# New orders of blocks in four feed-forward stages, free places asked for turned activations, earlier memory sums and shared keys and values stored in three parts

## The chip, the core and the metric

The kernel runs on one core of one Trainium2 chip. Its engines are PE (matrix products), DVE (vector), ACT (scalar), POOL (a slow general engine) and SP, which only issues DMA transfers, all on one queue and in program order. Each engine works off its own list of instructions in order and waits at the head of the list for what an instruction needs. The metric is the device time of one execution in microseconds (us); lower is better.

## What is computed

Two layers of a decoder trunk, with 256 tokens, width 1024 and 256 memory tokens. Each layer is a half-step SwiGLU feed-forward stage (FFN), a mixer, and a second FFN. Layer 0's mixer is an mLSTM with attention over the memory; layer 1's mixer (mixer B) is a dilated sliding-window attention with attention over the memory, and takes its keys and values from one projection made after layer 0.

```python
for layer in range(DEPTH):
    x = x + 0.5 * swiglu(rms_norm(x, ffn1_norm[layer]), ffn1_w_gate[layer], ffn1_w_up[layer], ffn1_w_down[layer])
    h = rms_norm(x, mix_norm[layer])
    mem_n = rms_norm(mem, mem_norm[layer])
    if layer < N_A_LAYERS:
        mix = mlstm_mixer(h, mem_n, ...)
    else:
        mix = dilated_mixer(h, mem_n, k_sh, v_sh, ...)
    x = x + mix
    x = x + 0.5 * swiglu(rms_norm(x, ffn2_norm[layer]), ...)
    if layer == N_A_LAYERS - 1:
        kv = rms_norm(x, kv_norm) @ w_kv
        k_sh, v_sh = ...
```

In `memory_cross_attention` the memory gives `kv = mem_n @ w_mem_kv`; the keys are normalised by head once more (`rms_norm` over 64 columns).

## The kernel before

**Products.** Every float32 matrix is split into a rounded high part `hi` and a remainder `lo`, and every product is three matmuls on PE: lo by high, hi by high, hi by low (`mm3`). The names show this: `gups<-lo,xh`, `gups<-hi,xh`, `gups<-hi,xl`. A token half is called t, 0 or 1.

**Weights.** They stream from DRAM in units of 128 x 1024 numbers (512 KB). SP loads a unit into one of six `raw` places, ACT casts it to `hi`, DVE subtracts it to `lo`; hi and lo stand in a ring of eight places until PE has used them. `_stream` writes down the order of the units for the whole kernel.

**FFN.** The hidden width 2816 makes eleven blocks of 256 columns. "g" with a block number is its gate and up products (into a bank of PSUM named `gups`, or `eb`, `gb`, `ub` where pieces are added up on DVE), "d" its product back to width 1024 (into `acc`). A step of two digits, such as 15 or 67, is one of seven products (first digit) of a scheme in the manner of Strassen that makes the gate and up products of two blocks, 5 and 6 or 7 and 8 (second digit 5 or 7), out of seven instead of eight; their weights are loaded as `pa` to `pd`, added and subtracted on DVE and split again, and their activations are `xs`, `xd`, `th`, `tl`. A "p" in the table is one row unit of `b_w_out` (mixer B's output matrix): it is split there, hi and lo go to DRAM as `wo`, and in mixer B two DMAs bring them back in place of a load, a cast and a subtraction.

**Turned blocks.** For d the activation `h` must stand with the hidden column on the partitions. For most blocks that is made without PE: DVE transposes h in squares of 32 into a place called `hb` (one instruction for each t), SP stores hb to DRAM (`hd`) and loads it back rearranged into a place called `ht`, then ACT casts it to `hhb` and DVE subtracts it to `hlb`, which PE reads. There are two hb places, one ht place and four places in DRAM. Both places are memory that a former user may still hold: an instruction that writes there waits for it, and holds up all behind it on its engine's list.

**Order.** `PLANS` gives the order of blocks for the four FFNs, named (layer, which): (0, 1), (0, 2), (1, 1), (1, 2). Within it the program is written by cooperative chains: each step of a chain is written down when a planner's clock, `_Model`, says that its inputs are ready on its engine; the planner's costs (`COST`, and in `_Engine` some special cases such as `pow` on POOL) decide only which instruction stands before which.

**Memory keys.** `memory_stats` loads the memory (`mt`), sums squares on ACT (`junk`) and takes the root on POOL (`memr`). `memory_kv` projects it (`mkvps`), scales by memr (`vm`, `sq` on ACT, `kn` on DVE), sums by head (`hss` on DVE), takes the root on POOL (`rp_e`, `rp_r`), multiplies kn by it on DVE and transposes it on PE (`tpk`). In layer 0 this is begun behind block 4 of FFN (0, 1).

**Shared keys and values.** `shared_kv` writes them to `kT` and `v` (traced as kTs and vs, 768 KB each); when all is done, `kept` stores both to DRAM with one DMA each, and mixer B loads them back. Their memory is used again by the next FFN, for hb among other things.

## Time and profile before

| | us |
|---|---|
| median of 3 runs | 989.51 (988.31 to 990.08) |
| the profiled execution | 989.23 |
| its span in the profile | 987.5 |
| PE busy in the span | 966.7 |
| DVE busy | 797.2 |
| ACT busy | 592.7 |

The profile lists for each engine the time in which it executes; in its timeline, matmuls of 512 columns are 0.39 us long and start 0.23 us apart, since they overlap. For an instruction that had to wait, the idle time ahead of it stands in brackets with the instruction that ended the wait.

The stages lie in the span as follows, read off the timeline: FFN (0, 1) to about 203, mixer A to 325, FFN (0, 2) to 501, the shared keys and values to 540, FFN (1, 1) to 731, mixer B to 793, FFN (1, 2) to the end.

### The profile page before, as it was taken

The numbers are of one execution on the slowest core, as the hardware profiler recorded it, in microseconds if no ns is written. First come the engines' busy times: TensorE is split into PE (matmuls) and PEld (weight loads), VectorE is DVE, ScalarE is ACT, GpSimd is POOL, SyncE is SP. The second block draws the span as 40 slices with busy tenths as digits, with TensorE's granted clock in tenths as the row PEclk, the third lists the DMA queues.
The fourth block names the chain that finished last, engine by engine and source line by source line (L and its number), as shares of the span: only waits on it lengthen the run. The fifth ranks groups of instructions, "written<-read, shape, count | busy, mean of one in ns | idle before, by whom it ended". The sixth has DMA issues, their size and how long they took to land.

```text
span 987.5 us, 13069 instructions
## 1 busy us (share of the span) xinstructions
PE 966.7 (98%) x4595; PEld 798.9 (81%) x4595; DVE 797.2 (81%) x1143; ACT 592.7 (60%) x931; POOL 49.6 (5%) x78
## 2 busy tenths in 40 slices
PE   9997999999999999999999999999999899999998
PEld 6886888899998888888878877778887678888877
DVE  5976976469896799999686799899676879898983
ACT  7664655377664756665476555665566476465651
POOL 0002000010010000000021000010002000000000
PEclk9999899999999999999999999999999999999999
DMA  9893278545455784843866866873757249468351
GB/s 355 297 384 144 86 235 298 166 146 199 128 192 193 293 302 157 304 173 121 291 186 181 324 233 226 277 271 97 258 201 262 89 165 336 159 221 313 105 182 54
DMA packets 82025, 212.40 MB, mean 215 GB/s; under 512 B 7788, under 2 KB 29224, under 8 KB 81960
## 3 DMA queue, kind: packets, MB, share of 16 engines
q1 hardware_dynamic: 81816, 211.54, 61.7%
q8 instruction: 36, 0.59, 0.2%
q14 instruction: 29, 0.24, 0.1%
q10 hardware_dynamic: 144, 0.04, 0.0%
HBM read 196.84 MB, written 14.70 MB: 214 GB/s over the span
## 4 chain that ended last, share of the span: by engine, by line
PE 73%; DVE 12%; DMA 6%; ACT 4%; issue 4%; POOL 1%; SPq 0%; DVEq 0%; ACTq 0%
PE gups L785 34%; PE acc L785 19%; DVE lo L369 6%; PE aps L785 6%; PE oacc L785 4%; PE kvps L785 3%; DMA ht<-hd 2%; DMA raw<-in_wts 2%; PE bqps L785 2%; ACT hi L369 1%; PE mkvps L785 1%; DMA kept<-vs 1%; PE tps L792 1%; DMA hd<-hb 1%; DVE hlb L369 1%
## 5 line engine op out<-in xcount | busy, mean ns | idle before, releaser
L369 DVE TENSOR_TENSOR lo<-raw,hi 128x1024 fp32r<-128x1024 f32 (+3 forms) x239 | 271.9, 1158 | 45.8 <-ACT hi L369 42.7
L369 ACT CAST hi<-raw 128x1024 fp32r<-128x1024 f32 (+3 forms) x239 | 232.9, 1002 | 50.7 <-PE gups L785 19.3
L785 PE MATMUL gups<-lo,xh 128*128 128x512 f32 x540 | 210.2, 392 | 2.8 <-DVE kn L369 1.9
L785 PE MATMUL gups<-hi,xh 128*128 128x512 f32 x540 | 209.5, 390 | 0.0
L785 PE MATMUL gups<-hi,xl 128*128 128x512 f32 x540 | 209.2, 390 | 0.0
L785 PEld LDWEIGHTS gups<-lo,xh 128*128 128x128 f32 x540 | 101.7, 188 | 25.5 <-DVE kn L369 2.3
L785 PE MATMUL acc<-lo,hhb 128*128 128x512 f32 x304 | 119.6, 393 | 0.5 <-ACT hhb L369 0.5
L785 PEld LDWEIGHTS gups<-hi,xh 128*128 128x128 f32 x540 | 101.4, 188 | 22.0 <-ACT hi L369 1.4
L785 PEld LDWEIGHTS gups<-hi,xl 128*128 128x128 f32 x540 | 101.5, 188 | 21.4
L785 PE MATMUL acc<-hi,hlb 128*128 128x512 f32 x304 | 118.6, 390 | 0.0
L785 PE MATMUL acc<-hi,hhb 128*128 128x512 f32 x304 | 118.3, 389 | 0.0
L369 DVE SCALAR_TENSOR_TENSOR lo<-raw,gains,hi 128x512 fp32r<-128x512 f32 x112 | 77.8, 744 | 9.2 <-ACT hi L369 8.6
L369 ACT ACTIVATE sil<-gups,rstd 128x256 f32<-128x256 f32 x67 | 31.6, 472 | 76.9 <-PE gups L785 76.7
L369 ACT ACTIVATE hi<-raw,gains 128x512 fp32r<-128x512 f32 x112 | 72.6, 713 | 6.0 <-DMA raw<-in_wts 2.2
L785 PEld LDWEIGHTS acc<-hi,hlb 128*128 128x128 f32 x304 | 57.1, 188 | 12.4 <-DVE hlb L369 0.4
L785 PEld LDWEIGHTS acc<-lo,hhb 128*128 128x128 f32 x304 | 57.1, 188 | 12.3 <-ACT hhb L369 0.9
L785 PEld LDWEIGHTS acc<-hi,hhb 128*128 128x128 f32 x304 | 57.1, 188 | 11.4
L369 ACT CAST hhb<-ht 128x512 fp32r<-128x512 f32 x38 | 23.5, 619 | 58.6 <-DMA ht<-hd 58.5
L785 PE MATMUL gups<-lo,th 128*128 128x512 f32 x136 | 54.2, 398 | 2.2 <-DVE gb L369 1.3
L369 DVE TENSOR_TENSOR lo<-pa,hi 128x1024 fp32r<-128x1024 f32 x42 | 51.1, 1216 | 5.3 <-ACT hi L369 4.9
L785 PE MATMUL gups<-hi,tl 128*128 128x512 f32 x136 | 53.8, 396 | 0.3 <-DVE tl L369 0.3
L785 PE MATMUL gups<-hi,th 128*128 128x512 f32 x136 | 53.7, 395 | 0.0
(237 smaller groups left out, 1594.5 us busy)
## 6 DMA issues: line engine op xcount, KB each, us to landing
raw<-in_wts SPq DMA_DIRECT2D x254, 512.0 KB, 5.2
raw<-in_wts SPq DMA_DIRECT2D x32, 384.0 KB, 3.8
hd<-hb SPq DMA_DIRECT2D x38, 256.0 KB, 5.1
ht<-hd SPq DMA_DIRECT2D x38, 256.0 KB, 4.6
pa<-in_wts SPq DMA_DIRECT2D x14, 512.0 KB, 5.1
pb<-in_wts SPq DMA_DIRECT2D x14, 512.0 KB, 6.1
pc<-in_wts SPq DMA_DIRECT2D x14, 512.0 KB, 7.0
pd<-in_wts SPq DMA_DIRECT2D x14, 512.0 KB, 5.9
```

The costliest lines, as they stand in the source:

```text
L369: call(out, *args, **kw)
L785: self.pe.matmul(out, lhsT=lhsT, rhs=rhs, start=start, stop=stop, skip_group_check=more)
L792: self.pe.transpose(out, in_, ident)
```

## The change

Five things are changed.

1. `PLANS` holds other orders for all four FFNs. Rows of `b_w_out` that are split early ("p") were two, one in (0, 2) and one in (1, 1); now they are six: one in (0, 1), four in (0, 2), one in (1, 1).
2. The hb and ht places: now two and two in (0, 1), two and one in (1, 1), three and two in the other two. A new `vacant` keeps a chain from writing down its transpose or its load until the planner holds the place to be free, and `held_by` counts the places in use. DRAM places are eight.
3. `memory_stats` for layer 0 is called behind block 2 of FFN (0, 1).
4. The planner's costs for POOL are larger: 0.5 instead of 0.24 for any instruction, 0.6 + 0.2 n instead of 0.4 + 0.07 n for pow.
5. `kept` stores in three parts: kT behind block 1 of the projection, and v for each t behind its block 2.

```diff
--- before.py
+++ after.py
@@ -47,14 +47,14 @@
 
 
 PLANS = {
-    (0, 1): "g0 g1 g2 d0 g3 g4 d2 d1 15 55 25 "
-            "65 d3 75 d4 45 35 g7 g8 d6 d5 g9 d7",
-    (0, 2): "g0 g1 g2 p d0 g3 d1 15 55 65 d2 25 75 d3 "
-            "45 35 g9 g4 d5 17 57 67 d6 77 27 47 37 d9 d4",
-    (1, 1): "g0 g2 g1 g3 d0 15 d1 55 65 d2 75 25 35 45 "
-            "g4 g9 17 p d3 d5 57 67 d4 77 27 47 d6 37 d9",
-    (1, 2): "g0 g1 g2 d0 g3 d1 15 55 65 d2 25 75 d3 45 "
-            "35 g9 g4 d5 17 57 67 d6 27 77 d4 47 37 d9",
+    (0, 1): "g0 g1 g2 g3 d0 g4 d2 d1 15 55 p 25 "
+            "65 d3 75 d4 45 35 g7 g8 g9 d5 d6 d7",
+    (0, 2): "g0 g1 g2 d0 p g3 15 55 p d1 65 d2 p 75 d3 25 "
+            "45 35 g9 g4 17 57 d6 67 d5 77 27 p 47 d9 d4 37",
+    (1, 1): "g0 g1 g2 g3 d0 d1 15 55 65 d2 75 25 35 45 "
+            "g4 g9 17 d3 d4 p 57 67 d5 77 27 47 d9 37 d6",
+    (1, 2): "g0 g2 g1 g3 d0 d1 15 55 65 25 75 d3 45 d2 "
+            "35 g9 g4 17 d6 57 67 d5 77 27 d4 47 d9 37",
 }
 
 
@@ -64,6 +64,7 @@
 
 LEAD = 3.0
 SOON = 8
+TURNING = {(0, 1): (2, 2), (1, 1): (2, 1)}
 SUMS = {(0, 1): 30.0, (0, 2): 16.0, (1, 1): 8.0, (1, 2): 8.0}
 EARLIER = 14
 
@@ -251,7 +252,7 @@
 class _Model:
 
 
-    COST = {"scalar": (0.03, 0.9e-3), "vector": (0.07, 1.04e-3), "gpsimd": (0.24, 0.8e-3)}
+    COST = {"scalar": (0.03, 0.9e-3), "vector": (0.07, 1.04e-3), "gpsimd": (0.5, 0.8e-3)}
     SAME = {"scalar": 0.1, "vector": 0.12, "gpsimd": 0.1, "tensor": 0.0, "sync": 0.0}
     CROSS = {("tensor", "scalar"): 0.2, ("tensor", "vector"): 0.2, ("scalar", "vector"): 0.13,
              ("scalar", "gpsimd"): 0.06, ("gpsimd", "vector"): 0.06, ("gpsimd", "scalar"): 0.06,
@@ -392,7 +393,7 @@
             if kw.get("accum_out") is not None or isinstance(kw.get("scale"), bass.AP):
                 cost += 0.09
             if name == "gpsimd" and ALU.pow in args:
-                cost = 0.4 + 0.07 * n
+                cost = 0.6 + 0.2 * n
             for a in args if method == "activation" else ():
                 table = model.TABLES.get(a) if isinstance(a, AF) else None
                 if table is not None and table != model.table:
@@ -543,6 +544,17 @@
 
         self.model.latest = max([self.model.latest] + [self.model.ready(a) for a in aps])
         yield
+
+    def vacant(self, pool, tag, bufs):
+
+        waited = 0.0
+        while True:
+            t = self.model.free((id(pool), tag), bufs)
+            if t <= max(self.now, waited):
+                return
+            waited = t
+            self.model.latest = max(self.model.latest, t)
+            yield
 
     def psum(self, pool, shape, name, reserved=False):
 
@@ -1017,7 +1029,14 @@
         nc = self.nc
         acc, chains, hT, blocks, made = [], {}, {}, {}, {}
         pairs = (layer, which) in PLANS
-        pending = set()
+        pending, turning, placing = set(), [0], [0]
+        HB, HT = TURNING.get((layer, which), (3, 2))
+
+        def held_by(count, most):
+
+            while count[0] >= most:
+                yield 0.05
+            count[0] += 1
 
         def room(*key):
 
@@ -1056,7 +1075,10 @@
                 h = self.work.tile([P, FB], F32, tag="ta", bufs=4, name="h")
                 yield from activated(ps, t, h)
                 if b not in blocks:
-                    blocks[b] = fp.tile([P, 4, 2, 2, 32], F32, tag="hb", bufs=2 if pairs else 1, name="hb")
+                    yield from self.vacant(fp, "hb", HB)
+                    yield from held_by(turning, HB)
+                if b not in blocks:
+                    blocks[b] = fp.tile([P, 4, 2, 2, 32], F32, tag="hb", bufs=HB, name="hb")
                 nc.vector.transpose(blocks[b][:, :, :, t, :].rearrange("p j c t -> p c j t"),
                                     h.rearrange("p (c j e) -> p c j e", c=2, j=4))
             return steps
@@ -1064,10 +1086,13 @@
         def placed(b, before):
             yield from self.wait(*before)
             hb = blocks.pop(b)
-            d = self.dram.tile([P, 512], F32, tag="hd", bufs=4, name="hd")
+            d = self.dram.tile([P, 512], F32, tag="hd", bufs=8, name="hd")
             nc.sync.dma_start(d, hb.rearrange("p j c t e -> p (j c t e)"))
+            turning[0] -= 1
             yield
-            ht = fp.tile([P, 4, P], F32, tag="ht", bufs=1, name="ht")
+            yield from self.vacant(fp, "ht", HT)
+            yield from held_by(placing, HT)
+            ht = fp.tile([P, 4, P], F32, tag="ht", bufs=HT, name="ht")
             nc.sync.dma_start(ht, bass.AP(d.tensor, d.offset, [[P, P], [32 * 512, 4], [1, P]]))
             yield
             yield from room(b, 1)
@@ -1075,6 +1100,7 @@
             hl = fp.tile([P, 4, 4, 32], F32R, tag="hl", bufs=4, name="hlb")
             yield from self.split(*(a.rearrange("p c i e -> p i c e") for a in (hh, hl)),
                                   ht.rearrange("p i (c e) -> p i c e", c=4))
+            placing[0] -= 1
             for t in range(2):
                 hT[b, t] = [tuple(a[:, 2 * c + t].rearrange("p i e -> p (i e)") for a in (hh, hl))
                             for c in range(2)]
@@ -1264,6 +1290,10 @@
                     follow(1, t, self.spawn(hidden(1, t)(ps[t])))
             elif step[0] == "memory":
                 memory()
+            elif step == ("gu", 2) and (layer, which) == (0, 1):
+                for t in range(2):
+                    gu(2, t)
+                self.memory_stats()
             elif step[0] == "st":
                 seventh(*step[1:])
             elif step[0] in ("gu", "dn"):
@@ -1737,18 +1767,20 @@
                     self.leave("tp")
             return steps
 
-        def kept(chains):
+        def kept(name, a, chains):
             yield from self.wait(*chains)
-            for a in (kT, v):
-                self.kept.append(self.dram.tile([P, 2 * MW], F32, name="kept"))
-                nc.sync.dma_start(self.kept[-1], a.rearrange("p a b -> p (a b)"))
+            self.kept[name] = self.dram.tile([P, a.free_size()], F32, name=f"kept{name}")
+            nc.sync.dma_start(self.kept[name], a)
 
         self.spawn(biases())
-        self.kept, chains = [], []
+        self.kept, chains = {}, []
         for b in range(3):
             for t in range(2):
                 chains.append(self.block(t, ("kv", b), 512, 2, taken(b, t)))
-        self.spawn(kept(chains))
+                if b == 2:
+                    self.spawn(kept(t, v[:, t, :], chains[2 + t::2]))
+            if b == 1:
+                self.spawn(kept("k", kT.rearrange("p a b -> p (a b)"), chains[:]))
 
     def mixer_b(self, after):
         nc, io = self.nc, self.io
@@ -1757,8 +1789,9 @@
             self.kT = mp.tile([P, 6, 256], F32, name="kTs")
             self.v = mp.tile([P, 2, MW], F32, name="vs")
             self.bias = mp.tile([P, 12, 256], F32, name="bias")
-            for a, kept in zip((self.kT, self.v), self.kept):
-                nc.sync.dma_start(a.rearrange("p a b -> p (a b)"), kept)
+            nc.sync.dma_start(self.kT.rearrange("p a b -> p (a b)"), self.kept["k"])
+            for t in range(2):
+                nc.sync.dma_start(self.v[:, t, :], self.kept[t])
             nc.sync.dma_start(self.bias, bass.AP(self.diag.tensor, self.diag.offset,
                                                  [[1, P], [384, 12], [1, 256]]))
             qg, mq = self.qg, self.mq[1]
@@ -1945,8 +1978,6 @@
         then = self.then
 
         def memory(layer, pool):
-            if layer == 0:
-                self.memory_stats()
             self.mem = self.memory_kv(layer, pool)
 
         with ExitStack() as ctx:
```

Three places show how the order of instructions moves.

DVE in FFN (0, 1) behind block 4, at layer 0's memory keys; numbers belong to buffers, hlb_983 and hlb_996 are turned blocks, kn_864 and kn_882 the first half of the memory keys. Before:

```order
L369 TENSOR_TENSOR lo36_932<-pd0_770,hi36_931 128x1024
L369 TENSOR_TENSOR pd0_770<-pd0_770,pa0_542 128x1024
L369 TENSOR_SCALAR kn_879<-mkvps_824,memr1_91 128x256
L369 TENSOR_TENSOR hlb_952<-ht_822,hhb_951 128x4x4x32
L369 TENSOR_TENSOR hlb_983<-ht_939,hhb_982 128x4x4x32
L369 TENSOR_REDUCE hss_993<-sq_969 128x4
L369 TENSOR_TENSOR kn_864<-kn_864,rp_r_948 128x256
L369 TENSOR_TENSOR lo37_1007<-pd2_788,hi37_1006 128x1024
L369 TENSOR_TENSOR lo38_1010<-pa0_542,hi38_1009 128x1024
L369 TENSOR_TENSOR pd2_788<-pd2_788,pa2_631 128x1024
L369 TENSOR_TENSOR pb0_633<-pc0_695,pb0_633 128x1024
L369 TENSOR_TENSOR lo39_1013<-pa2_631,hi39_1012 128x1024
```

After the change:

```order
L370 TENSOR_REDUCE hss_932<-sq_909 128x4
L370 TENSOR_TENSOR lo34_925<-pa0_677,hi34_924 128x1024
L370 TENSOR_TENSOR pa0_677<-pc0_714,pa0_677 128x1024
L370 TENSOR_TENSOR lo35_961<-pa2_696,hi35_960 128x1024
L370 TENSOR_TENSOR pa2_696<-pc2_774,pa2_696 128x1024
L370 TENSOR_TENSOR lo36_964<-raw36_781,hi36_963 128x1024
L370 TENSOR_TENSOR kn_882<-kn_882,rp_r_904 128x256
L370 TENSOR_TENSOR lo37_967<-pd0_806,hi37_966 128x1024
L370 TENSOR_TENSOR pd0_806<-pd0_806,pa0_677 128x1024
L370 TENSOR_TENSOR kn_907<-kn_907,rp_r_935 128x256
L370 TENSOR_TENSOR hlb_996<-ht_958,hhb_995 128x4x4x32
L370 TENSOR_TENSOR lo38_1018<-pd2_830,hi38_1017 128x1024
```

The two multiplies of kn by rp_r stand ahead of the hlb split now and close together; before, two hlb splits and hss stood ahead of the first, and the second stood eight rows further on.

SP at the end of FFN (0, 2), with the two turned blocks that are used last: hd stores a block, ht loads it back, raw is a weight unit. Before:

```order
L369 DMA hd_4596<-hb_4509 128x512
L369 DMA raw198_4602<-in_wts 128x1024
L369 DMA ht_4613<-hd_4559 128x4x128
L369 DMA raw199_4625<-in_wts 128x1024
L369 DMA raw200_4628<-in_wts 128x1024
L369 DMA raw201_4643<-in_wts 128x1024
L369 DMA raw202_4656<-in_wts 128x1024
L369 DMA ht_4667<-hd_4596 128x4x128
```

After the change:

```order
L370 DMA ht_4657<-hd_4597 128x4x128
L370 DMA raw204_4660<-in_wts 128x1024
L370 DMA raw205_4678<-in_wts 128x1024
L370 DMA raw206_4684<-in_wts 128x1024
L370 DMA hd_4714<-hb_4543 128x512
L370 DMA raw207_4723<-in_wts 128x1024
L370 DMA ht_4756<-hd_4714 128x4x128
```

The last of these blocks (block 8: hd_4596, then hd_4714) had six entries between its store and its load and now has one. On PE the number of matmuls of 512 columns between the last one of that block's gate and up products and the first that reads its hhb is 108 before and 60 after. For block 1 of FFN (1, 2) it is 120 and 72, and for its block 8 it is 84 and 60; the smallest number before is 60, for the last turned block but one of the kernel.

DVE in mixer B, at the scores of the second token half: qn is a query, s a score, nmb its largest value, xl a remainder that the output product reads. Before:

```order
L369 TENSOR_TENSOR lo310_7363<-raw310_7166,hi310_7362 128x1024
L369 TENSOR_TENSOR xl0_7131<-po_7346,xh0_7130 128x3x128
L369 TENSOR_REDUCE hss_7392<-sq_7367 128x8
L369 SCALAR_TENSOR_TENSOR s_7414<-pa_7410,rqb1_7038,bias_7031 128x256 x2
L369 SCALAR_TENSOR_TENSOR s_7414<-pa_7412,rqb1_7038,bias_7031 128x256
L369 SCALAR_TENSOR_TENSOR s_7415<-pa_7411,rqb1_7038,bias_7031 128x256 x2
L369 SCALAR_TENSOR_TENSOR s_7415<-pb_7413,rqb1_7038,bias_7031 128x256
L369 TENSOR_REDUCE nmb_7443<-s_7414 128x1
L369 TENSOR_REDUCE nmb_7445<-s_7415 128x1
L369 TENSOR_TENSOR lo311_7432<-raw311_7168,hi311_7431 128x1024
L369 TENSOR_TENSOR lo312_7435<-raw312_7170,hi312_7434 128x1024
L369 TENSOR_TENSOR xl0_7131<-po_7422,xh0_7130 128x256
```

After the change:

```order
L370 TENSOR_SCALAR qn_7408<-bqps_7290,rstd_7066 128x512
L370 TENSOR_REDUCE hss_7425<-sq_7409 128x8
L370 TENSOR_TENSOR lo315_7420<-raw315_7335,hi315_7419 128x1024
L370 TENSOR_TENSOR lo316_7449<-raw316_7337,hi316_7448 128x1024
L370 SCALAR_TENSOR_TENSOR s_7466<-pa_7454,rqb1_7081,bias_7073 128x256 x2
L370 SCALAR_TENSOR_TENSOR s_7466<-pa_7456,rqb1_7081,bias_7073 128x256
L370 SCALAR_TENSOR_TENSOR s_7467<-pa_7455,rqb1_7081,bias_7073 128x256 x2
L370 SCALAR_TENSOR_TENSOR s_7467<-pb_7465,rqb1_7081,bias_7073 128x256
L370 TENSOR_REDUCE nmb_7493<-s_7466 128x1
L370 TENSOR_REDUCE nmb_7495<-s_7467 128x1
L370 TENSOR_TENSOR xl0_7174<-po_7478,xh0_7173 128x256
```

The pair of lo splits ahead of xl0 stands ahead of the scores now; the splits lo309 and lo310 (and lo307 and lo308, further up) are gone, since those four rows come from DRAM already split. On PE, the pa products that make s stand behind the output products (oacc) of three rows of b_w_out, where they stood ahead of them.

## The prediction

> **What bounds the kernel now.** I read the page's busy rows first, then the table of who waited for whom on PE, then windows of the stretches where PE stands.
>
> ```profile
> span 987.5 us, 13069 instructions
> PE 966.7 (98%) x4595; PEld 798.9 (81%) x4595; DVE 797.2 (81%) x1143; ACT 592.7 (60%) x931; POOL 49.6 (5%) x78
> ...
> PE 73%; DVE 12%; DMA 6%; ACT 4%; issue 4%; POOL 1%; SPq 0%; DVEq 0%; ACTq 0%
> ```
>
> PE, the matrix engine, is busy for 966.7 of 987.5 us. The change leaves its 4595 matmuls alone, so all that can be won is the 20.8 us in which PE stands, and any stretch in which it runs slowly. The profiled execution took 989.23 us, 1.73 us more than its span and 0.28 us less than the median of 989.51 us, far inside what I can resolve. I add my terms to 989.23.
>
> ```profile
> PE tpk L792 <- DVE kn L369: 4.6, 1, 4.6
> PE gups L785 <- DVE kn L369: 2.7, 2, 1.9
> PE oacc L785 <- DVE xl L369: 2.3, 1, 2.3
> PE tpq L792 <- DVE qn L369: 1.7, 1, 1.7
> PE gups L785 <- DVE gb L369: 1.3, 1, 1.3
> ...
> PE tps L792 <- ACT mp L369: 0.6, 1, 0.6
> PE acc L785 <- ACT hhb L369: 0.5, 1, 0.5
> PE gups L785 <- DVE h L369: 0.5, 1, 0.5
> ...
> PE po L785 <- ACT mp L369: 0.4, 1, 0.4
> ```
>
> Columns: total, times, longest. Three groups matter: kn (normalised memory keys) in layer 0; kn, gb and h in the first FFN of layer 1; qn and xl in mixer B. The next windows give PE's busy time, then the loads, DVE, ACT, POOL, the granted clock, the DMA share and GB/s.
>
> ```profile
> 92.00:102.00 10.00, 4.71 (x13) 3.59 (x14) 6.27 (x9) 5.26 (x7) 2.17 (x2) 0.75 0.09 26
> ...
> 325.00:501.00 176.00, 176.00 (x787) 145.69 (x786) 153.15 (x189) 106.40 (x144) 2.03 (x5) 1.00 0.66 230
> ...
> 575.00:650.00 75.00, 70.70 (x305) 56.20 (x304) 70.17 (x94) 46.17 (x68) 2.22 (x2) 1.00 0.68 241
> ```
>
> In FFN (1,1), from 575 to 650, DVE has 70.17 of 75: it is in arrears there. FFN (0,2), 325 to 501, has no idle PE at all, so it has nothing to give and can only lose.
>
> **A. Layer 0's memory sums, and the places for turned blocks: -7.5 us.**
>
> ```profile
> 91.25 0.39 PE L785 MATMUL gups<-hi,xh 128*128 128x512 f32 x1
> 91.48 0.39 PE L785 MATMUL gups<-hi,xl 128*128 128x512 f32 x1
> 92.67 0.47 PE L785 MATMUL gups<-lo,th 128*128 128x512 f32 x1 [0.81 <-DVE kn L369]
> ...
> 98.22 0.69 PE L792 MATMUL tpk<-consts,kn 128*128 128x128 f32 x2 [4.62 <-DVE kn L369]
> ...
> 99.56 0.63 PE L785 MATMUL gups<-hi,tl 128*128 128x512 f32 x1
> 99.99 0.63 PE L785 MATMUL gups<-lo,th 128*128 128x512 f32 x1
> ```
>
> PE idles 0.81 + 4.62 = 5.43 us. After the long gap matmuls start 99.99 - 99.56 = 0.43 us apart instead of 91.48 - 91.25 = 0.23, and 0.75 is the mean granted clock of the window. In the timeline 12 matmuls, from 98.56 to 103.40, go by at that pace: 12 x 0.20 = 2.4 us. So the place costs 7.8 us. What kept kn:
>
> ```profile
> 90.51 0.56 POOL L369 TENSOR_TENSOR memr<-memr,mhalf 128x1 f32<-128x1 f32 x1
> ```
>
> ```profile
> 92.04 0.48 DVE L369 TENSOR_SCALAR kn<-mkvps,memr 128x256 f32<-128x256 f32 x1 [1.78 <-ACT sq L369]
> ...
> 96.81 0.69 DVE L369 TENSOR_TENSOR hlb<-ht,hhb 128x512 fp32r<-128x512 f32 x1 [3.69 <-ACT hhb L369]
> 97.42 0.41 DVE L369 TENSOR_REDUCE hss<-sq 128x4 f32<-128x256 f32 x1
> 97.75 0.42 DVE L369 TENSOR_TENSOR kn<-kn,rp_r 128x256 f32<-128x256 f32 x1
> ```
>
> The factor memr of the second memory half is ready at 91.07. Then DVE stands 3.69 us at an hlb split whose block came through the single ht place, and only behind it does the row's kn multiply stand. Both go: the sums are made after block 2, some 30 us of matmuls earlier, so both memr precede the key products, and in the new DVE order the kn multiplies stand ahead of that hlb. There are two ht places here too. What is late next is DVE itself: with the pause gone, its splits behind block 4 have no 4.6 us in which to catch up. I leave 0.3 us for that (bounds 0 and 1.5): 7.8 - 0.3 = 7.5. The two mem loads move ahead of the stream of weights; no idle PE lies in the 20 us of matmuls that follow, and the weights they pass are used over 10 us after their splits in the new order, so I cost them at nothing; without that cover they cost 1.05 MB at 330 GB/s (a row under B), 3.2 us.
>
> The Trainium skill, "TensorE: Matmul & The Clock Gate", section "HAM oscillation — how this bites in real kernels", says that an idle gap above about 3.4 us halves the clock until the engine has been busy again for as long. The trace agrees: 0.43 against 0.23 us after 4.62 us, and no such change after 0.81 us.
>
> **B. Keys and values stored in three parts; FFN (1,1): -3.2 us.**
>
> ```profile
> 548.87 0.45 DVE L369 STREAM_TRANSPOSE hb<-h 128x256 f32<-128x256 f32 x1 [4.74 <-DMA kept<-vs]
> ```
>
> ```profile
> 538.89 9.86 DMA kept<-vs
> ```
>
> ```profile
> 538.00:549.00 11.00, 11.00 (x50) 9.13 (x49) 2.83 (x6) 5.24 (x10) 0.00 (x0) 1.00 0.96 330
> ```
>
> hb reuses the memory of kT and v, so DVE stands 4.74 us until their stores have landed, 9.86 us after issue, in a stretch where the DMA engines are 0.96 busy. The last store is now 384 KB instead of 768 KB and is issued ahead of the 512 KB part that stood before it; kT's 768 KB go earlier. That takes at least 0.9 MB from ahead of its end: 0.9 MB / 330 GB/s = 2.7 us sooner, and up to 5.0 us if kT has left the queue. The issue itself still waits for ACT's last vs. So DVE wins 2.7 to 4.7 us. PE idles 75 - 70.70 = 4.3 us from 575 to 650 (kn 1.9, gb 1.3, h 0.5 and less), all on DVE results, in a chain of arrears that starts here. DVE's arrears shrink by 2.7 us or more, but the order of blocks brings other splits late, so I give three quarters: 3.2 us. Bounds 0 and 4.3.
>
> **C. Four more rows of b_w_out split early; mixer B: -2.0 us.**
>
> ```profile
> 766.05 2.35 DVE L369 TENSOR_TENSOR lo<-raw,hi 128x1024 fp32r<-128x1024 f32 x2
> ...
> 773.14 1.80 DVE L369 TENSOR_REDUCE nmb<-s 128x1 f32<-128x768 f32 x2
> 774.86 2.35 DVE L369 TENSOR_TENSOR lo<-raw,hi 128x1024 fp32r<-128x1024 f32 x2
> 777.13 0.42 DVE L369 TENSOR_TENSOR xl<-po,xh 128x256 fp32r<-128x256 f32 x1
> ```
>
> PE waits 2.33 us for this xl and 1.70 for qn. Four splits of about 1.16 us leave this stretch of DVE and four casts leave ACT; the pair directly ahead of xl (2.35 us) is now ahead of the scores. But the pa products move behind the earlier oacc products, some 2 us later on PE, so 2.35 - 2 = 0.35 us of xl's wait goes for sure, and all of it at best. qn waited for ACT's sq, which has four casts less ahead: I take 1.4 of 1.70. With 0.6 for xl: 2.0 us. Bounds 0.4 and 4.0. The tps and po waits on mp (1.0 us) keep their order and stay. The six stored pairs are read back by DMA just ahead, where there is room:
>
> ```profile
> 744.00:793.00 49.00, 43.43 (x298) 32.69 (x296) 38.51 (x84) 28.34 (x67) 5.99 (x6) 1.00 0.47 172
> ```
>
> Six pairs of 1.05 MB are 6.3 MB, 19 us of full queues at 330 GB/s, against two pairs before and four weight units of 512 KB that are no longer read here. If that came late, PE would wait for hi; I keep it inside C's lower bound.
>
> **D. What the new orders cost: +3.0 us.**
>
> ```profile
> L369 DVE TENSOR_TENSOR lo<-raw,hi 128x1024 fp32r<-128x1024 f32 (+3 forms) x239 | 271.9, 1158 | 45.8 <-ACT hi L369 42.7
> ...
> L369 ACT CAST hi<-raw 128x1024 fp32r<-128x1024 f32 (+3 forms) x239 | 232.9, 1002 | 50.7 <-PE gups L785 19.3
> ...
> ht<-hd SPq DMA_DIRECT2D x38, 256.0 KB, 4.6
> ```
>
> (0,2) gets three more split rows, 3 x 1.16 = 3.5 us of DVE and 3.0 of ACT. 153.15 + 3.5 of 176 still fits on average, hidden under matmuls; with that cover gone it is 3.5 us. The sharper matter is the turned blocks. Between the last gate-and-up matmul of block 8 and the first that reads its hhb, the old order of (0,2) has 108 matmuls of 512 columns, the new one 60: 60 x 0.227 = 13.6 us for the activation, two DMAs through DRAM and the split. The old kernel has such a gap of 60 once, at the end, and there PE waited the 0.5 us of the row for hhb, with this landing of hd, and these of ht, first at the end and then in (0,2), 470 to 505:
>
> ```profile
> 952.79 4.95 DMA hd<-hb
> ```
>
> ```profile
> DMA to landing us min/median/max: 2.9/2.9/2.9
> ```
>
> ```profile
> DMA to landing us min/median/max: 6.7/6.7/6.7
> ```
>
> With the median 4.6 the wait near 487 us is 0.5 + 4.6 - 2.9 = 2.2 us; with 6.7 it is 4.3; with 2.9, 0.5. I take 2.2, the page's median over 38. Block 1 of (1,2) goes from 120 to 72 matmuls, 2.7 us more room than 60: no wait at the median. Its block 8 goes from 84 to 60 at the quiet end: 0.5. For values of h and lo that now come within 1 us of their matmul in (0,2) and (1,2), 0.3. Sum 3.0, bounds 0.5 and 7. The larger cost of pow in the planner adds no instruction, and so nothing of its own.
>
> The Trainium skill, "DMA: Bandwidth & Descriptors", table of two cost components, has about 2.0 us fixed plus bytes at 436 GB/s, an estimate of 2.6 us for 256 KB. The measured median is 4.6, so the measurement decides; by the page's figure the wait near 487 would be 0.2 us and the sum 977.5.
>
> **Sum.** -7.5 - 3.2 - 2.0 + 3.0 = -9.7; 989.23 - 9.7 = 979.5 us.
>
> **Rivals.**
> 1. All listed waits go and none comes: 7.8 + 4.3 + 4.0 + 0.5 = 16.6, hence 972.6. For it: at the three places the missing operand has less DVE work queued ahead of it. Against it: mixer B's scores themselves come later, and D's gaps are shorter than any the old kernel hid.
> 2. Only A goes. DVE is the engine in arrears in (1,1) (70.17 of 75) and total DVE work is unchanged; the waits of B and C then reappear at other operands, and D grows from 3 to 4 us: 989.2 - 7.5 + 4 = 985.7.
> 3. A doesn't do what it says, since kn meets another hold (a late mem load, or the sums themselves behind splits on ACT): 979.5 + 7.5 = 987.
> 4. Slower. The turned blocks near 487 us and in (1,2) meet full DMA queues: if hd and ht both land at 6.7 us, against 4.9 and 2.9 where the 60 matmuls cost 0.5 us, PE stands 0.5 + 5.6 = 6.1 us at the gap of 60 and 6.1 - 2.7 = 3.4 at that of 72. If both gaps are long enough to be followed by a slow stretch like that at 99 us (2.4 each), they cost 14.3; with the 0.5 at the end, 989.2 - 12.7 + 14.8 = 991.3. With both slow stretches it breaks even where the two landings take together 12.4 us instead of 4.95 + 2.9; the rows so far show 6.7 for a single one.
>
> That slow stretch is what the clock gate page of the Trainium skill, same section as above, predicts for gaps above 3.4 us; one gap in this trace shows it.
>
> **How the numbers follow.** The forecast (976 to 983) has 0.55, rival 1 (972 to 976) 0.14, rival 2 (983 to 987) 0.17, rival 3 0.05, rival 4 0.05, and 0.04 is left for gains that cancel exactly. The range 972 to 987 takes in rivals 1 and 2 and the bounds of the terms. A measurement of this kernel can tell about 0.2%, 2 us, from no change. Faster by more: 0.55 + 0.14 + 0.17 and 0.03 of rival 3, 0.89; same 0.02 + 0.04 = 0.06; slower 0.05.
>
> **What would show it.** A: no tpk wait near 98 us and a granted clock of 1.00 from 85 to 105. B: DVE's wait for the kept store below 2 us, PE's idle in (1,1) below 1.5 us. C: no tpq wait, an oacc wait of 1 to 2 us. D: an acc wait for hhb of some 2 us at the end of (0,2), ahead of no other new wait over 1 us. The forecast is wrong if PE idles over 4 us in one piece anywhere, or if (1,1) still idles 4 us.

## The result and the profile after

The changed kernel took 974.11 us in the median of four runs (972.51 to 974.86), against 988.91 us (987.62 to 990.08) for the kernel before on the same chip: a ratio of 0.9848, with a 95% interval of 0.983 to 0.9867. That is 14.8 us less; 979.5 with a range of 972 to 987 was forecast, so the gain came out half as large again as predicted. The execution that was profiled has a span of 973.1 us, 14.4 us less than before.

First the page of the changed kernel: span, PE's line, and the first shares of the chain that ended last.

```profile
span 973.1 us, 13107 instructions
PE 963.5 (99%) x4595; PEld 797.2 (82%) x4595; DVE 798.0 (82%) x1143; ACT 594.5 (61%) x931; POOL 47.3 (5%) x78
...
PE 80%; DVE 10%; DMA 5%; issue 2%; ACT 2%; SPq 0%; DVEq 0%; ACTq 0%
```

PE stands 973.1 - 963.5 = 9.6 us instead of 20.8. Its matmuls are as many as before; its busy time is 3.2 us less: 2.4 us of that is the slow pace of 12 matmuls, which is gone, and the rest is spread over several stages. Next, whom PE waits for (total, times, longest):

```profile
PE gups L797 <- DVE ub L370: 1.4, 1, 1.4
PE warm L1944 <- DVE warm L370: 1.2, 1, 1.2
PE acc L797 <- DVE hlb L370: 0.8, 1, 0.8
PE gups L797 <- DVE lo L370: 0.7, 2, 0.4
PE oacc L797 <- DVE xl L370: 0.6, 1, 0.6
PE gups L797 <- DVE gb L370: 0.5, 1, 0.5
PE po L797 <- ACT mp L370: 0.4, 1, 0.4
PE tps L804 <- ACT mp L370: 0.3, 1, 0.3
```

tpk for kn and tpq for qn are gone from the list, xl is down from 2.3 to 0.6 us, and no wait is longer than 1.4 us.

Where the time went is seen best by stage. The table is read off PE's timeline: each stage runs from its first matmul to the first of the next, and the last one to the start of the last matmul. By this, mixer B ends at 807.8 us before, and not at 793 as in the list ahead of the prediction; it is 76.5 us long. "Again" is a second profile of the changed kernel, taken with later runs.

| stage | before | changed | again | change | forecast |
|---|---|---|---|---|---|
| FFN (0,1) | 200.5 | 193.1 | 192.3 | -7.4 | A: -7.5 |
| mixer A | 119.7 | 119.7 | 119.5 | 0.0 | |
| FFN (0,2) | 176.5 | 177.9 | 178.2 | +1.4 | D: +2.2 and part of 0.3 |
| keys and values | 35.7 | 35.8 | 35.8 | +0.2 | |
| FFN (1,1) | 193.8 | 189.8 | 189.4 | -3.9 | B: -3.2 |
| mixer B | 76.5 | 71.5 | 71.5 | -5.1 | C: -2.0 |
| FFN (1,2) | 176.2 | 176.5 | 175.9 | +0.2 | D: +0.5 and part of 0.3 |

Four windows, of PE's busy time, the loads, DVE, ACT, POOL, granted clock, DMA share and GB/s, stand for A, (0,2), (1,1) and mixer B:

```profile
85.00:105.00 20.00, 19.85 (x89) 15.78 (x88) 19.90 (x22) 13.50 (x18) 1.69 (x1) 1.00 0.36 113
318.00:496.00 178.00, 177.16 (x790) 145.86 (x790) 157.29 (x193) 109.16 (x148) 1.74 (x4) 1.00 0.73 255
568.00:643.00 75.00, 73.28 (x322) 59.66 (x321) 71.13 (x95) 48.08 (x70) 4.31 (x4) 1.00 0.67 234
721.50:793.00 71.50, 70.14 (x447) 54.58 (x446) 51.33 (x107) 42.61 (x95) 9.69 (x12) 1.00 0.60 221
```

The same of the kernel before, for (0,2) and mixer B:

```profile
325.30:501.80 176.50, 176.50 (x790) 146.03 (x789) 153.85 (x190) 106.90 (x145) 1.73 (x4) 1.00 0.66 230
731.30:807.80 76.50, 70.93 (x446) 54.84 (x445) 55.65 (x111) 45.91 (x99) 9.66 (x12) 1.00 0.51 179
```

At the memory keys (85 to 105) DVE is busy for 19.90 of 20 us and PE has no pause and its full clock. In (1,1) PE idles 1.7 of 75 us, where it idled 4.3. In (0,2) DVE has 157.29 us of work instead of 153.85, the 3.5 us that the three early rows cost. In mixer B PE idles 1.4 us instead of 5.6.

The three hits and the one miss in lines. At the memory keys, PE's timeline now runs through tpk:

```profile
92.85 0.39 PE L797 MATMUL gups<-hi,tl 128*128 128x512 f32 x1
93.08 0.38 PE L804 MATMUL tpk<-consts,kn 128*128 128x128 f32 x2
93.22 0.48 PE L797 MATMUL gups<-lo,th 128*128 128x512 f32 x1
```

In FFN (1,1), DVE's timeline at its first transpose:

```profile
538.69 0.45 DVE L370 STREAM_TRANSPOSE hb<-h 128x256 f32<-128x256 f32 x1 [0.48 <-DMA kept<-vs]
```

4.74 us of waiting for the stores have become 0.48. In mixer B, DVE's timeline ahead of the xl that PE waits for:

```profile
757.32 1.23 DVE L370 TENSOR_TENSOR lo<-raw,hi 128x1024 fp32r<-128x1024 f32 x1 [0.94 <-ACT hi L370]
758.46 2.05 DVE L370 SCALAR_TENSOR_TENSOR s<-pa,rqb,bias 128x256 f32<-128x256 f32 x5
760.42 0.48 DVE L370 SCALAR_TENSOR_TENSOR s<-pb,rqb,bias 128x256 f32<-128x256 f32 x1
760.82 1.80 DVE L370 TENSOR_REDUCE nmb<-s 128x1 f32<-128x768 f32 x2
762.54 0.41 DVE L370 TENSOR_TENSOR xl<-po,xh 128x256 fp32r<-128x256 f32 x1
```

From the first score to the end of xl these are 762.95 - 758.46 = 4.5 us without a gap. Before, from 769.38 to 777.55, it was 8.2 us: besides the pair of splits (2.35) a wait for POOL stood among the scores. The row of the kernel before:

```profile
771.57 1.27 DVE L369 SCALAR_TENSOR_TENSOR s<-pa,rqb,bias 128x256 f32<-128x256 f32 x3 [1.32 <-POOL rqb L369]
```

And block 8 of (0,2), the miss. The block's last product on PE, then the load of ht on SP, which issued hd at 469.80, then ACT and PE:

```profile
466.25 0.39 PE L797 MATMUL gups<-hi,tl 128*128 128x512 f32 x1
```

```profile
475.29 0.38 SPq L370 DMA_DIRECT2D ht<-hd  x1
```

```profile
478.85 0.61 ACT L370 CAST hhb<-ht 128x512 fp32r<-128x512 f32 x1
```

```profile
480.14 0.39 PE L797 MATMUL gups<-hi,xl 128*128 128x512 f32 x1
480.36 0.39 PE L797 MATMUL acc<-lo,hhb 128*128 128x512 f32 x1
```

The trace's figures for the two ht loads between 440 and 500 us; the first took 6.5 us to land, this one 2.8:

```profile
DMA to landing us min/median/max: 2.8/4.7/6.5
```

The cast ends at 479.46 and PE reads it at 480.36 with no idle time in front. The gap of 60 matmuls was long enough by 0.9 us. Two things made it so. The load landed in 2.8 us. And the block was with SP sooner: hd was issued 3.6 us behind the start of the block's last product. At the gap of 60 in the kernel before, from which the forecast took its 0.5 us, that was 5.9 us, from this row to the issue at 952.79:

```profile
946.92 0.39 PE L785 MATMUL gups<-hi,xl 128*128 128x512 f32 x1
```

### The profile page after: what moved, and what is told of

It is laid out like the page before. It is cut to its first block, busy times and chain, and to the rows that moved or that the text cites. A ratio compares the mean times of both kernels' runs of the same rounds, so it can differ in the third digit from the quotient of the medians.

```text
span 973.1 us, 13107 instructions
## 1 busy us (share of the span) xinstructions
PE 963.5 (99%) x4595; PEld 797.2 (82%) x4595; DVE 798.0 (82%) x1143; ACT 594.5 (61%) x931; POOL 47.3 (5%) x78
## 4 chain that ended last, share of the span: by engine, by line
PE 80%; DVE 10%; DMA 5%; issue 2%; ACT 2%; SPq 0%; DVEq 0%; ACTq 0%
PE gups L797 36%; PE acc L797 20%; PE aps L797 8%; DVE lo L370 6%; PE oacc L797 4%; PE kvps L797 3%; DMA raw<-in_wts 3%; PE mkvps L797 2%; PE bqps L797 2%; DMA hd<-hb 1%; PE tps L804 1%; ACT hi L370 1%; DMA ht<-hd 1%; DMA xraw<-in_xT 1%; PE sc L797 1%
## 5 line engine op out<-in xcount | busy, mean ns | idle before, releaser
L370 DVE TENSOR_TENSOR lo<-raw,hi 128x1024 fp32r<-128x1024 f32 (+2 forms) x239 | 272.6, 1159 | 52.1 <-ACT hi L370 49.6
L370 ACT CAST hi<-raw 128x1024 fp32r<-128x1024 f32 (+2 forms) x239 | 234.5, 1002 | 55.4 <-PE gups L797 18.7
L370 ACT CAST hi<-pa 128x1024 fp32r<-128x1024 f32 x42 | 43.5, 1051 | 17.3 <-DVE pa L370 11.5
```

What stands on the lines that cost most here:

```text
L370: call(out, *args, **kw)
```

## Experiments

In the first nine runs one part of the change was undone in the changed kernel, or made alone in the kernel before. Each was timed once, beside runs of the kernel before: 989.6 us for late sums, old stores, two early rows and old places; 986.9 us for early sums, six early rows, old orders and old costs; 988.5 us (median of 7) for the new stores alone. All runs of the kernel before lie between 986.3 and 991.8 us, so that a single time beside them tells little of differences of 3 us or less; therefore stages are compared, with the table above. The planner writes everything behind an edit down anew, so that small moves elsewhere are part of each result. How far a stage moves by itself was seen too: two profiles of the changed kernel differ by 0.8 us in (0,1), mostly in its first 10 us, and in the run with the old stores below (0,2) was 1.3 us longer although DVE's order there is the same.

**The memory sums late again.**

```diff
-            elif step == ("gu", 2) and (layer, which) == (0, 1):
-                for t in range(2):
-                    gu(2, t)
-                self.memory_stats()
...
         def memory(layer, pool):
+            if layer == 0:
+                self.memory_stats()
```

> The changed kernel with the memory sums of layer 0 made behind block 4 again, as before. If the early sums are what removed the wait for the memory keys, PE stands again 4 us or more at tpk, FFN (0,1) is 5 to 8 us longer than its 193.1 us from the first gate product to the first product of mixer A, and the kernel takes about 980 us. Rival: the second ht place and the planner's larger POOL costs removed it, by taking the hlb split out of the way of kn; then the sums may be late without harm, FFN (0,1) stays within 1.5 us of 193.1 and the kernel at about 974.

979.94 us; FFN (0,1) took 199.0 us, 5.9 more. The first theory holds for the time, but not for the place: PE waited not at tpk but at weight splits. DVE stood 3.39 us for memr, but that is not in the chain that ends PE's first wait. The chain goes from DVE's split at 96.23 to ACT's cast for it, and that stood behind a copy of eb for which ACT had waited 4.30 us until PE was there. So the late sums cost 5.9 us here on another path than in the kernel before; how they bring about that order on ACT stays open. DVE's timeline, then ACT's, then PE's:

```profile
89.01 0.48 DVE L370 TENSOR_SCALAR kn<-mkvps,memr 128x256 f32<-128x256 f32 x1 [3.39 <-POOL memr L370]
...
96.23 1.22 DVE L370 TENSOR_TENSOR lo<-pd,hi 128x1024 fp32r<-128x1024 f32 x1 [1.95 <-ACT hi L370]
```

```profile
94.67 0.59 ACT L370 COPY eb<-gups 128x512 f32<-128x512 f32 x1 [4.30 <-PE tpk L804]
```

```profile
97.52 0.50 PE L797 MATMUL gups<-lo,xh 128*128 128x512 f32 x1 [2.18 <-DVE lo L370]
...
99.91 0.80 PE L797 MATMUL gups<-lo,xh 128*128 128x512 f32 x1 [0.73 <-DVE lo L370]
100.50 0.63 PE L797 MATMUL gups<-hi,xh 128*128 128x512 f32 x1
100.93 0.63 PE L797 MATMUL gups<-hi,xl 128*128 128x512 f32 x1
```

These are 2.9 us of idle PE, and the slow pace (0.43 us between starts) of 13 matmuls makes about as much again.

**The early memory sums alone**, the same lines added to the kernel before.

> The kernel before with one thing changed: the memory sums of layer 0 made behind block 2. If late sums alone made the wait of 5.4 us and the slow stretch behind it, FFN (0,1) falls from 200.5 to 193 to 194 us and the kernel takes 982 to 983. Rival: the single ht place, which holds the hlb split ahead of kn, is as much to blame; then a wait of 2 us or more for kn stays at tpk, FFN (0,1) takes 196 us or more and the kernel 985 or more.

979.89 us, 7.0 less than the run of the kernel before beside it and 9.0 less than the 988.91 above. FFN (0,1) took 191.0 us, 9.5 less than before: about 0.5 us of it in the first 10 us, 8.5 at the memory keys and just behind. That is all of A and more. All other stages stayed within 0.3 us. The single ht place did no harm by itself. DVE's timeline of this run:

```profile
84.66 0.42 DVE L369 TENSOR_TENSOR kn<-kn,rp_r 128x256 f32<-128x256 f32 x1
85.00 0.68 DVE L369 TENSOR_TENSOR hlb<-ht,hhb 128x512 fp32r<-128x512 f32 x1
```

The hlb splits no longer wait. In the kernel before they had only passed a delay on: memr late, so sq and kn late, so the hlb behind kn late, so the one ht place freed late, so the next hlb late, and behind it the multiply of kn.

**The stores as before.** `kept` as in the old lines of the diff: one chain behind the whole projection, two DMAs of 768 KB.

> The changed kernel with keys and values stored by two DMAs of 768 KB behind the whole projection, as before. If these stores held DVE and its arrears made PE wait in FFN (1,1), DVE waits again 3 us or more at its first transpose there, FFN (1,1) is 2 to 4 us longer than its 189.8 us and the kernel takes 976 to 978 us. Rival: the new order of blocks in (1,1) gives the gain and has room for the wait; then DVE waits 3 us or more, but PE's idle time in (1,1) grows by less than 1 us and the kernel takes 974 to 975.

977.14 us. DVE waited 5.78 us at its first transpose, and (1,1) took 191.6 us, 1.8 more; PE's waits there grew from 1.7 to 2.9 us, the one for ub to 1.96. Neither theory's numbers are met in full: the stores are worth 1.8 us in this order, a third of what they cost DVE. The other 1.3 us of the difference stand in (0,2), ahead of the edit.

**The stores in three parts, alone.**

> The kernel before with one thing changed: keys stored behind block 1 of the projection, values for each token half behind its block 2. If the late stores began the arrears of DVE in FFN (1,1), DVE's wait at its first transpose there falls from 4.74 us to below 2, PE's waits in (1,1) fall by 2 us or more from 4.0, and the kernel takes 985 to 987 us. Rival: the old order of blocks gives the time back at its own tight places (gb near 608, kn near 644); then DVE's wait falls but PE's waits in (1,1) stay above 3 us and the kernel at 988 to 990.

986.67 us, against 986.3 to 991.8 for the seven runs of the kernel before beside it, so that the total decides nothing. DVE did not wait for the stores at all, but (1,1) gained only 1.5 us of the 4.74. The wait for gb near 608 became one for ub (1.16), and kn, 1.93 before, became 0.73 and 1.33 at two places: PE's waits sum to 3.6 us, close to the rival. So the stores alone move the waits more than they remove them.

**Two early rows instead of six.** In `PLANS` the "p" of (0,1) and three of (0,2) taken out.

```diff
-    (0, 1): "g0 g1 g2 g3 d0 g4 d2 d1 15 55 p 25 "
+    (0, 1): "g0 g1 g2 g3 d0 g4 d2 d1 15 55 25 "
...
-    (0, 2): "g0 g1 g2 d0 p g3 15 55 p d1 65 d2 p 75 d3 25 "
-            "45 35 g9 g4 17 57 d6 67 d5 77 27 p 47 d9 d4 37",
+    (0, 2): "g0 g1 g2 d0 p g3 15 55 d1 65 d2 75 d3 25 "
+            "45 35 g9 g4 17 57 d6 67 d5 77 27 47 d9 d4 37",
```

> The changed kernel with two rows of b_w_out split early instead of six (one in (0,2), one in (1,1), everything else as changed). If the four rows were what held mixer B, mixer B, from its first query product to the first gate product of the last FFN, takes 3 us or more above its 71.5 us (76.5 before the change), with waits for xl and qn back, and FFN (0,2) is up to 1 us shorter than its 177.9. Rival: mixer B's gain comes from the planner's POOL costs, which moved the scores behind the output products; then mixer B stays below 73 us.

978.57 us; mixer B took 75.7 us, 4.2 more, with 2.66 us of PE waiting for s; the waits for xl and qn that were expected did not come back. The rows are the main part of C. FFN (0,2) did not get shorter but 2.1 us longer (180.0): without three of its splits PE waited 1.08 and 1.51 us for h at two places. The waits of the run (PE):

```profile
PE tpp L804 <- DVE s L370: 2.7, 1, 2.7
PE tph L804 <- DVE h L370: 1.5, 1, 1.5
...
PE gups L797 <- DVE h L370: 1.1, 1, 1.1
```

**Six early rows in the old orders**, four "p" added to the old `PLANS`: one in (0,1) behind 55, three in (0,2), behind 55, d2 and 27.

> The kernel before with one thing changed: six rows of b_w_out split early instead of two, in the old orders of blocks (one in (0,1), four in (0,2), one in (1,1)). If DVE's and ACT's splits are what hold mixer B, it falls from 76.5 to about 72 us. If early splits cost their stage the time that they take on DVE, FFN (0,2) grows by up to 3.5 us from 176.5; if they are hidden there, it grows by less than 0.5. Sum: 985 (hidden) to 989 (not hidden).

992.56 us, past the worst case that was expected: 5.7 more than the kernel before beside it, but the stages sum to 3.2 more than in the profile before. Mixer B fell to 72.5 us, a gain of 4.0. But (0,2) grew by 4.6 us (waits of 1.03 for ub, 1.08 for h and 1.02 for hhb), (1,1) by 1.6, (1,2) by 0.4. A split of 1.2 us costs its stage more than itself here. That this is because it makes turned blocks late that go through few places is argued, not shown by this run.

**Old places and no asking**, everything else as changed: two hb, one ht, four DRAM places, `vacant` and `held_by` not called.

> The changed kernel with two hb places, one ht place, four DRAM places and no asking for a free place, as before; orders, sums, stores and costs as changed. If the places bring gain of their own, ACT and DVE stand for hhb and hlb as in the old kernel, and PE's waits grow by 3 us or more, in (0,2) and (1,2) where three and two places were given: about 977 to 980 us. Rival: the orders of blocks and the sums carry the gain, and the places none that PE sees: within 1.5 us of 974.

979.72 us. (0,2) took 181.4 us, 3.5 more, with new waits of 1.14 for h and 1.13 for ub; (1,1) 1.5 more, (1,2) 0.7 more. So in the new orders the places, or the asking, are what lets (0,2) bear four early rows; the run undoes both and does not part them.

**Old orders of blocks**, the old `PLANS` in the changed kernel, with its two early rows.

> The changed kernel with the old orders of blocks, old places of the two early rows among them; sums, places, stores and costs as changed. If the new orders carry gain beyond the four early rows, the kernel takes more than the 978.6 of the changed kernel with two early rows: 980 to 983, with waits in FFN (1,1). Rival: the orders themselves are worth nothing, only the four rows are: within 1.5 us of 978.6.

980.78 us. (0,2) took 176.5 us, with its one early row, and (1,1) 190.1, about as in the new orders; mixer B 75.7, by the four rows. The other loss is not in (1,1), where it was expected, but in (1,2): 180.9 us, 4.4 more, with 1.08 us for h and 1.32 for hhb in a row at its end and the slow pace behind them. So the gain of (1,1) is not in its order of blocks, and (1,2) needs its new one once the places are changed.

**The planner's old POOL costs**, 0.24 and 0.4 + 0.07 n.

> The changed kernel with the planner's old, smaller costs for POOL. If the planner's error on POOL mattered, instructions that wait for a root on POOL (kn in (0,1) and (1,1), scores in mixer B) stand too early in DVE's order, DVE waits for POOL there by 2 us or more in all, and the kernel takes 1 to 3 us more than 974. Rival: with the sums early nothing near POOL is tight: within 1 us of 974.

976.96 us: 1.0 us more in mixer B, where the wait for s (0.43) came back and that for xl rose to 1.00; 1.1 us more in (0,2), about 0.4 in each of (0,1) and (1,2); 0.8 less in (1,1). At this size the differences outside mixer B can't be told from the moves of a stage by itself.

**Closeness in the order.** The last three ran on one chip, timed four times each: the changed kernel again, and two kernels with other orders of (1,1) and (1,2).

```diff
-    (1, 1): "g0 g1 g2 g3 d0 d1 15 55 65 d2 75 25 35 45 "
-            "g4 g9 17 d3 d4 p 57 67 d5 77 27 47 d9 37 d6",
-    (1, 2): "g0 g2 g1 g3 d0 d1 15 55 65 25 75 d3 45 d2 "
-            "35 g9 g4 17 d6 57 67 d5 77 27 d4 47 d9 37",
+    (1, 1): "g0 g1 g2 g3 d0 15 55 d1 65 d2 75 25 35 45 g4 g9 17 d3 d4 p 57 67 d5 77 27 47 d9 37 d6",
+    (1, 2): "g0 g2 g1 d0 g3 d1 15 55 65 25 75 d3 45 d2 35 g9 g4 17 d6 57 67 d5 77 27 d4 47 d9 37",
```

The second has the same (1, 2) and, in (1, 1), this line:

```diff
+    (1, 1): "g0 g1 g2 g3 d0 d1 15 55 65 75 25 d2 35 45 g4 g9 17 d3 d4 p 57 67 d5 77 27 47 d9 37 d6",
```

> The changed kernel itself, once more, as the measure for the two below on the same chip: 974 us, 0.985 of the kernel before.

> The changed kernel with two other orders of blocks: in (1,1) the down product of block 0 stands ahead of 15 and that of block 1 behind 55, in (1,2) g0 g2 g1 d0 g3 d1 opens and d2 stays where it was. In the new order no lo, ub or gb is written down within 1 us of its matmul where PE waited 1.4, 0.4 and 0.5 us; one tl near the start of (1,1) is. If such closeness in the order is what leaves waits, 1 to 2 us less than the changed kernel: 972 to 973. Rival: DVE is as far in arrears in (1,1) as its work makes it, and the wait only moves: within 0.7 us of the changed kernel.

> As the kernel before it in this list, with another order in (1,1): d2 behind 25 instead of behind 65, d0 and d1 as in the changed kernel. Here one gb in the middle of (1,1) is close to its matmul and nothing else: 1 to 2 us less than the changed kernel if closeness decides, within 0.7 us of it if the arrears do.

973.28 us for the changed kernel (0.9847 of before, 0.9822 to 0.9871), 972.77 for the first (0.9847, 0.9816 to 0.9879) and 977.92 for the second (0.9894, 0.9869 to 0.9918). The first lost the waits for ub, lo and gb and got one of 0.73 us for tl: 0.8 us less in (1,1), and nothing that the timing can tell. The second shows how little closeness says about size. It was expected that one gb would be close to its matmul, and nothing else, and that this would cost little; PE waited 4.57 us for that gb, and the kernel took 4.6 us more. PE's timeline, then DVE's ahead of it:

```profile
598.24 0.80 PE L795 MATMUL gups<-lo,th 128*128 128x512 f32 x1 [4.57 <-DVE gb L368]
598.83 0.63 PE L795 MATMUL gups<-hi,th 128*128 128x512 f32 x1
```

```profile
595.11 1.22 DVE L368 TENSOR_TENSOR lo<-pd,hi 128x1024 fp32r<-128x1024 f32 x1
596.36 1.23 DVE L368 TENSOR_TENSOR pd<-pd,pa 128x1024 f32<-128x1024 f32 x1
597.50 0.69 DVE L368 TENSOR_TENSOR gb<-gups,eb 128x512 f32<-128x512 f32 x1
```

DVE works without a gap for over 15 us ahead of that gb: the arrears of the whole stretch come due at the one operand that stands last. No version clearly better than the changed kernel was found.

## Why the prediction was right, step by step

**What bounds.** The pool was right: PE's matmuls stayed, and the gain came out of PE's 20.8 us of idle time (11.2) and out of PE's busy time (3.2, of which the slow pace is 2.4). The time of 974.1 us lies below the 976 to 983 of the forecast, in the band of rival 1.

**A (forecast -7.5, stage -7.4).** The place, the size and the clock at it were right. One step was wrong: "Both go", the sums and the places, was given as two causes. The early sums alone give all of it in the kernel before (-9.5 in the stage), and with two ht places but late sums 5.9 us come back. The ht place was a link in the chain, not a cause. That 7.4 came so near to 7.5 is in part luck, for the early sums are worth more than was forecast. Some 0.6 us of the 9.5 is now lost in (0,1) to its early row: against the kernel with two early rows, PE falls behind by that much between 99 and 106 us.

**B (-3.2, stage -3.9).** The step that the store's wait of DVE falls by 2.7 to 4.7 us was right: 4.74 to 0.48. The step from there to PE ("I give three quarters") held for the stage only by sum. The stores are worth 1.5 us alone and 1.8 in the changed kernel; the places are worth 1.5 in this stage; the order of blocks, nothing. Each of these is near the 1.3 us by which a stage moved by itself. So that the stage met the forecast is luck: about half of its gain came from the places, to which B gave no price.

**C (-2.0, stage -5.1).** Right in kind, too small by more than half, and this is most of what the forecast missed. The failing step is the 0.6 us for xl: it set 2 us for the scores' later place against 2.35 us of splits and left out the 1.32 us in which DVE waited for POOL's rqb among those very scores. With the scores later, rqb was ready, and the wait of 2.33 fell to 0.59. That wait for rqb is gone in the kernel with six early rows in the old orders too, where xl's wait was 1.0 us and one split still stood between the scores and xl; so the rows alone remove it. Of the tps and po waits, 0.3 us went too, and PE's wait for s (0.43) went wholly. The stage's 5.1 us are 4.2 of idle time and 0.8 of PE's busy time; the cause of the 0.8 stays open. By experiment, the four rows make 4.2 of the 5.1 us (two rows instead of six), the POOL costs about 1.0. Such sums of single steps need not add up. The prediction put the POOL costs at "nothing of its own", since they add no instruction; 1.0 us in mixer B is what that left out.

**D (+3.0, stages +1.6).** The step that failed is the 2.2 us at block 8 of (0,2), "With the median 4.6": ht landed in 2.8 us, near the 2.9 of the reference instead of the median, with a single weight load between hd and ht on the queue. That alone would leave about 0.9 us of wait, an estimate from the prediction's own sum: 0.5 + 0.5 - 0.1, as ht was issued 5.5 us behind hd where the reference's hd took 4.95 to land. What made the wait vanish is a step that the prediction took to be the same: from the block's last product to its store it was 2.3 us shorter here. The wait that did come, 0.84 us for an hlb at 390.6, belongs to the 0.3 us set aside for close operands. The three early rows of (0,2) are hidden in that order with its places, as was costed, but in the old orders and places the same rows cost 4.6 us. Whether order or places decide was not parted: six rows in the old orders with the new places were not run.

**The signs.** Those of A came true: no wait at tpk, and a clock of 1.00 from 85 to 105. Of B's, DVE's wait fell below 2 us, but PE idles 1.7 us from 568 to 643, not below 1.5. Of C's, the wait for qn is gone, but xl's is 0.59 instead of 1 to 2. Of D's, neither came true: there was no wait for hhb, and one of 1.36 for ub was over 1 us. Neither sign of a wrong forecast came.

**Rivals.** The first, that all listed waits go and none comes, forecast 972.6 and came nearest to the time, but not by its mechanism: 0.59 us for xl stayed, 1.36 for ub and 0.84 for hlb came, and 0.8 us came from busy time in mixer B instead. That only A goes was refuted by mixer B; that A fails, by tpk. The slower case needed landings of 6.7 us at gaps of 60; the load there landed in 2.8. A long idle gap with a slow stretch behind it did appear, but at a gb and in a kernel of the experiments (4.57 us, then 0.43 us between starts).

## What to carry to other kernels

When an engine stands at a long chain, test the head of the chain alone before crediting its links: one early sum gave all that the place for a buffer seemed to share. Work that is moved to a stage with room on average is not free: with three more splits (0,2) is 1.4 us longer in the new order with more places, 4.9 in that order with the old places, and 4.6 in the old order with the old places. And when a consumer's wait is estimated from what is queued ahead, the waits inside that queue count as well as the work.

## What was not expected of the hardware

PE's slow pace came after shorter gaps than 4.6 us. All single idle times of 2.43 us and more in these runs were followed by starts 0.43 us apart: 2.43 us (six rows in the old orders), 2.65 (old orders) and 2.66 (two rows) are the shortest. Below that it is mixed: 2.18 us with late sums were followed by it, where the granted clock fell at 99.03, between that gap and the one of 0.73 behind it, and so was a pair of 1.08 and 1.32 us (old orders); single gaps of 2.33 us (old mixer B, in three runs) and 1.93 us were not. The Trainium skill, "TensorE: Matmul & The Clock Gate", section "HAM oscillation — how this bites in real kernels", names gaps above about 3.4 us; the runs here show the slow pace from some 2.2 us on, below 2.4 us not always.

How long it lasts varies as well: after the same wait of 4.6 us at tpk, starts 0.43 us apart lasted until 103.8 us in the profile before, and until about 101 us in the kernel with the stores in three parts, whose order there is the same. The granted clock (third number from the end) was 0.50 for 6.83 us in the one and 3.41 us in the other, and every slow stretch of these runs behind their first 10 us and ahead of their end has one of these two lengths:

```profile
97.08:103.91 6.83, 5.69 (x15) 4.53 (x16) 6.83 (x9) 4.34 (x6) 2.17 (x2) 0.50 0.00 0
```

```profile
97.67:101.08 3.41, 2.89 (x8) 2.40 (x9) 3.41 (x5) 3.41 (x6) 2.17 (x2) 0.50 0.00 0
```

So the 2.4 us that the prediction counted for the slow stretch is one of two values that this place showed, and its "The trace agrees" holds for the halving of the clock, not for how long that lasts.

POOL's small operations are not of one length in the profile: the same rp_r of 128 x 4 took 1.01 to 1.88 us, and memr's product 0.56 or 1.43 us. POOL's lines for rp_r in the run with late sums:

```profile
85.99 1.01 POOL L370 TENSOR_TENSOR rp_r<-rp_e,mhalf 128x4 f32<-128x4 f32 x1
...
93.28 1.88 POOL L370 TENSOR_TENSOR rp_r<-rp_e,mhalf 128x4 f32<-128x4 f32 x1
```
